# A hybrid decoder layer on one core: weight splits three chunks ahead and behind the background steps, new first and last jobs, mLSTM gates moved up

## The chip, the cores and the metric

The kernel runs on one core of one Trainium2 chip. The metric is the time of one execution on the device in microseconds; each kernel is executed several times and the median is compared.

## The reference

One inference step of one decoder layer for 256 prompt tokens and 64 sample tokens (8 sequences of 8), 320 columns in all, D = 2048, float32. Cut to what matters here:

```python
def trunk(x, ...):
    for l in range(DEPTH):                                   # DEPTH = 1
        x = x + 0.5 * swiglu(rmsnorm(x, ln_ffa[l]), w_ffa_in[l], w_ffa_out[l])   # D_FF = 5632
        y, st_new = token_mixer(rmsnorm(x, ln_mix[l]), w_in[l], ...)
        x = x + y
        x = x + 0.5 * swiglu(rmsnorm(x, ln_ffb[l]), w_ffb_in[l], w_ffb_out[l])
    return rmsnorm(x, ln_f), stacked

def token_mixer(h, ...):
    qk_pre, mv, mo, mif, aq, ak, av, gm, ga = split_cols(h @ w_in)
    qk, conv_new = causal_conv(qk_pre, conv_buf, conv_w, conv_b)      # then SiLU: mLSTM q and k
    hm, (C1, n1, m1) = mlstm(mq, mk, mv, ig, lf, C0, n0, m0)          # ig, lf from mif
    hm = sigmoid(mo) * rms(hm) * m_norm
    ha = dilated_attention(aq, ak, av, caches, biases)
    merged = sigmoid(gm) * (hm @ w_pm) + sigmoid(ga) * (ha @ w_pa)
    return merged @ w_out, new_states
```

Beside the output it returns the new keys and values, the mLSTM states and the convolution rows.

## The kernel before, in words

Activations stand feature-major: a tile holds 2 x 128 features by 320 tokens. Every weight is used once, so each product of the layer is a stream of weights through TensorE with 320 columns of activations. To keep float32 accuracy both operands are split into two reduced-precision parts, `hi` and `lo`, and each product becomes three: hi with x's high part, hi with x's low part, lo with x's high part (L144 is the helper `mm` that issues them, so all matmuls have that line; L332 is the transpose helper).

The work is a list of jobs (`add_job`), each one block of 256 output features over all its k-tiles, accumulated in a PSUM pair `fg` (two buffers). A job is cut into *chunks* of four k-tiles (512 KB of weights), numbered through the program as `ci`. The order of the jobs: first feed-forward (in blocks of 12, 12, 10 and 10 k-tiles: gate and up jobs, then eight output jobs), the mixer's projections (attention q, k, v of head pairs; the gate job `mif`, which is a single chunk with 8 columns; then for each mLSTM head v, q, k and the output gate `mo`; then 16 jobs of the branch gates), the two branch projections (`pm`, `pa`), the output projection, and the second feed-forward.

`run_job` issues a job chunk by chunk. For chunk ci it does, in this order: `split_upto(ci + HLB)`, which has ACT cast raw to `hi` (L223) and DVE subtract to `lo` (L224); one step of the background generators in the list `even` or `odd` (every second chunk each), of `slow` (8 of 15 chunks) and of `every`; the job's `setup`; in the first chunk `flush_evac`, which starts the evacuation of the job before and puts what is left of it (after its first `yield`) into `every`; `load_upto`, which issues the weight DMAs on SP; and then the chunk's 24 products. So evacuations, attention, mLSTM and conversions stand as small steps between the chunks, on all engines, and each engine works in the order of the program. HLB = 3 buffers of hi and lo and RAWB = 4 of raw mean: at chunk ci chunk ci+2 is split, into the buffer of chunk ci-1, and the load of chunk ci+6 is issued, into the buffer of chunk ci+2.

The background generators that matter here: `sample_attention` (`slow`: it transposes cache keys `kraw` on DVE into `kd`, L631, and multiplies with small matmuls), `prompt_attention` (`even`), `mlstm` (`odd`: `load_head`, `prep`, `front`, `update`, then four times `retrieve` and `state`, then `numer`), `mif_evac` (a chain of operations on 4 partitions, L814 to L876), `mv_evac`, `ak_evac`, `av_evac` (L395 `times_rstd` on DVE, then after two yields six transposes and copies: `tok_major`), `qk_evac`, and `sigmoid_evac` (DVE multiply L395, ACT exp L954, POOL add L955, and DVE reciprocals L958 after a `yield` each). `take` splits the branch results of the four heads into `bh` and `bl` (L1301, L1302) at the first `pm` and `pa` job, the first head's being made ahead by `presplit`.

The start: `load_x` and `load_upto` load four pieces of x (512 KB and the sample rows) and the first chunks in turn on SP; `prep_pair` transposes 256 features of x, and makes high and low parts with the gain; `first_chunk` places the pairs before and inside the first three chunks, with eight warm-up matmuls (`warm(8)`) before the first product. The end: the last job's evacuation, square sums over tokens by matmuls with ones (`token_sums`), square root and reciprocal, six transposes, and the scaling of the output `Y` (L1595 on ACT, L1597 on DVE), stored in six DMAs on SP.

Of the kernel before, what the change touches and what calls it, by code (L numbers as in the profile page):

```python
# [128 lines left out]
def decoder_kernel(tc, I, O, K):  # L129
# [55 lines left out]
    RAWB, HLB, KRB = 4, 3, 3  # L185
# [84 lines left out]
    def run_job(job):  # L270
        cs, nkt, mov, evac, kind, setup = job
        ps = fg_tile()
        for n, (ci, k0, nk) in enumerate(cs):
            run_later()
            if ci < 5:
                first_chunk(ci, 0)
            else:
                split_upto(ci + HLB)
# [10 lines left out]
            if n == 0 and setup is not None:  # L289
                setup()  # L290
            if ci == 7 or (n == 0 and ci != 4):
                flush_evac()
            load_upto(ci + HLB + RAWB)
            h, l = wh.pop(ci), wl.pop(ci)
            for m in range(1 if kind == "mif" else 2):
                if m and ci < 3:
                    first_chunk(ci, 1)
# [107 lines left out]
    xl = {}  # L405

    def load_x(c):
        xl[c] = fp.tile([128, 3, 512], F32, tag="xl", bufs=3, name="xl")
        G.memset(xl[c][64:128, 2], 0.0)
        dma(xl[c][:, 0:2], I["x_prompt"][0].rearrange("(t p) d -> p t d", p=128)[:, :, c * 512:(c + 1) * 512])  # L410
        dma(xl[c][0:NS, 2], I["x_sample"].rearrange("b t d -> (b t) d")[:, c * 512:(c + 1) * 512])
# [194 lines left out]
    def sample_attention():  # L606
# [145 lines left out]
        for u in range(17):  # L752
# [6 lines left out]
            if u:  # L759
                if u % 4 == 1:  # L760
                    o4 = mxt([128, 4, 128], "o", 2, "osb")
# [42 lines left out]
    def mif_evac(ps):  # L804
# [5 lines left out]
        rst = mp_tile("rst")[0:4, :, 0:NT]  # L810
# [156 lines left out]
    def mlstm():  # L967
# [229 lines left out]
        for h in range(4):  # L1197
            for s4 in range(4):
# [13 lines left out]
                elif h < 3:  # L1212
# [68 lines left out]
    add_job(w_in, 0, 16, C_MIF, mov_x, mif_evac, kind="mif")  # L1281
# [25 lines left out]
    def presplit(key):  # L1307
        while key not in M:
            yield
        PRE[key] = split_act(M[key][0], t_tile)  # L1310

    def take(key):
        for h in range(4):
            BH[h], BL[h] = PRE[key] if h == 0 and key in PRE else split_act(M[key][h], t_tile)
# [83 lines left out]
    def token_sums(x):  # L1398
        ps = bg_tile()
        for t, t0 in enumerate(TOK):  # L1400
            for m in range(2):
                mm(ps[:, t:t + 1], x[:, m, t0:t0 + 128], ones[:, 0:1], m == 0, m == 1)
        return ps


    def ffb_last(ps, j):
# [3 lines left out]
        if j < 7:  # L1410
            V.scalar_tensor_tensor(X[j], ps[:, :, 0:NT], 0.5, X[j], op0=OP.mult, op1=OP.add)
            sumsq(X[j], j, p)
        else:
            Y["sq"] = ft_tile("sq")
            for m in range(2):
                V.scalar_tensor_tensor(X[j][:, m], ps[:, m, 0:NT], 0.5, X[j][:, m], op0=OP.mult, op1=OP.add)
                S.activation(Y["sq"][:, m], X[j][:, m], AF.Square)
# [5 lines left out]
        if j < 7:  # L1423
            yield
        if j == 6:
            pa_ = token_sums(state["ss"])
            V.tensor_copy(rt, pa_[:, 0:3])
# [25 lines left out]
    vps = bg_tile()  # L1453
    tr(vps[:, 0:16], vffa)
    V.tensor_copy(gv[:, 0:16], vps[:, 0:16])

    def prep_pair(j, fg=False):
# [3 lines left out]
        ft = fg_tile() if fg else None  # L1461
        ps = [ft[:, 0], ft[:, 1]] if fg else [bg_tile(), bg_tile()]
# [4 lines left out]
        V.tensor_copy(X[j][:, 1], ps[1][:, 0:NT])  # L1467
        for m in range(2):
            S.activation(XH[j][:, m], ps[m][:, 0:NT], AF.Copy, scale=gv[:, g0 + m:g0 + m + 1])
            if m == 0:  # L1470
                S.copy(X[j][:, 0], ps[0][:, 0:NT])
        for m in range(2):
            V.scalar_tensor_tensor(XL[j][:, m], ps[m][:, 0:NT], gv[:, g0 + m:g0 + m + 1],
                                   XH[j][:, m].bitcast(F32), op0=OP.mult, op1=OP.subtract)

    def first_chunk(n, m):
        if n == 0 and m == 0:
            prep_pair(0)
            prep_pair(1)
            split_upto(1)  # L1480
            prep_pair(2, True)
            warm(8)
        elif n < 3:
            prep_pair(2 * n + 2 + m)
            if m == 1:
# [147 lines left out]
```

## Time and profile before

| | us |
|---|---|
| runs of the kernel before: median (lowest to highest) of 3 | 2980.31 (2979.14 to 2981.5) |
| the profiled execution's own time | 2975.59 |
| its span | 2973.8 |
| busy in it: PE / DVE / ACT / POOL | 2924.8 / 1637.5 / 1087.8 / 226.0 |
| mean granted clock of TensorE | 0.995 |
| DMA, mean over the span | 187 GB/s |

A page or an answer of the trace gives times from the span's start in microseconds, and mean durations in nanoseconds. "PE" is the matmuls, "PEld" the weight loads, which overlap them. In a timeline a row is: start, duration, engine, line, operation, output<-inputs, shape, how many were merged, and in brackets the idle time of the engine before it with what ended it. In a group row it is: busy us, mean ns of one, then idle time before and what ended it.

### The profile page before, as it was taken

Reading aid. Unit: us, or ns where it says so; the run is one execution under the profiler, and the core shown is the slowest. Engines: PE = TensorE matmul, PEld = TensorE weight load, DVE = VectorE, ACT = ScalarE, POOL = GpSimd, SP = SyncE. Lnnn points to the kernel's source line nnn. Section 1 sums busy time; section 2 is a strip of 40 time slices with the busy share of each in tenths; the row PEclk is TensorE's granted clock in tenths of the full one; section 3 lists DMA queues with packets and bytes.
Section 4 is the critical chain, followed back from the end, with each engine's and each line's share of the span. In section 5 each row is a group of like instructions: output and inputs, shape, how many; then the busy total and the mean of one; then the engine's idle time right before and its main releaser. Section 6 shows DMA issues by size and latency. Waiting matters only on the chain.

```text
span 2973.8 us, 51323 instructions
## 1 busy us (share of the span) xinstructions
PE 2924.8 (98%) x21538; PEld 2875.4 (97%) x21538; DVE 1637.5 (55%) x1939; ACT 1087.8 (37%) x1359; POOL 226.0 (8%) x256
## 2 busy tenths in 40 slices
PE   9999999999999999999999999999999999999998
PEld 8999999999999999988889999999999999999998
DVE  6444444444446556878888875654444444444444
ACT  5332333333334333433443443334333333333334
POOL 1000000000000000122222210000000000000000
PEclk9999999999999999999999999999999999999999
DMA  6454444444546788898999986554444444445443
GB/s 195 151 159 155 149 149 149 149 150 143 158 145 184 224 231 248 223 296 272 301 282 313 308 275 218 184 176 152 150 149 149 149 149 150 151 146 156 149 141 115
DMA packets 507477, 557.23 MB, mean 187 GB/s; under 512 B 30125, under 2 KB 452061, under 8 KB 507221
## 3 DMA queue, kind: packets, MB, share of 16 engines
q1 hardware_dynamic: 507068, 553.87, 61.2%
q8 instruction: 169, 2.77, 0.4%
q14 instruction: 64, 0.52, 0.1%
q10 hardware_dynamic: 176, 0.07, 0.0%
HBM read 521.58 MB, written 32.28 MB: 186 GB/s over the span
## 4 chain that ended last, share of the span: by engine, by line
PE 50%; DMA 1%; DVE 1%; issue 0%; ACT 0%; DVEq 0%; SPq 0%; ACTq 0%
PE fg L144 47%; PE bg L144 3%; PE bg L332 0%; DMA raw<-in_w_in_dram 0%; DMA vt<-in_cache_v_dram 0%; DMA k<-qk_d 0%; DMA raw<-in_w_pm_dram 0%; DVE kd L631 0%; DVE lo L224 0%; DVE pre L928 0%; ACT hi L223 0%; DVE sg L958 0%; DVE vs L1073 0%; DVE Y L1597 0%; DVE bl L1302 0%
## 5 line engine op out<-in xcount | busy, mean ns | idle before, releaser
L224 DVE TENSOR_TENSOR lo<-raw,hi 128x1024 fp32r<-128x1024 f32 (+1 forms) x784 | 969.1, 1237 | 1204.2 <-ACT hi L223 1189.9
L144 PE MATMUL fg<-xh,hi 128*128 128x320 f32 x4240 | 1323.0, 312 | 2.6 <-ACT hi L223 2.6
L144 PE MATMUL fg<-xh,lo 128*128 128x320 f32 x4240 | 1314.3, 310 | 8.6 <-DVE lo L224 8.6
L144 PE MATMUL fg<-xl,hi 128*128 128x320 f32 x4240 | 1313.0, 310 | 0.0
L223 ACT CAST hi<-raw 128x1024 fp32r<-128x1024 f32 (+1 forms) x784 | 806.3, 1029 | 1356.7 <-PE fg L144 1014.2
L144 PEld LDWEIGHTS fg<-xh,lo 128*128 128x128 f32 x4240 | 797.4, 188 | 11.7 <-DVE lo L224 11.5
L144 PEld LDWEIGHTS fg<-xh,hi 128*128 128x128 f32 x4240 | 797.9, 188 | 5.7 <-ACT hi L223 3.1
L144 PEld LDWEIGHTS fg<-xl,hi 128*128 128x128 f32 x4240 | 797.8, 188 | 1.0 <-issue 0.2
L144 PE MATMUL fg<-hh,hi 128*128 128x320 f32 x1408 | 437.0, 310 | 0.0
L144 PE MATMUL fg<-hl,hi 128*128 128x320 f32 x1408 | 435.2, 309 | 0.0
L144 PE MATMUL fg<-hh,lo 128*128 128x320 f32 x1408 | 435.2, 309 | 0.0
L144 PEld LDWEIGHTS fg<-hl,hi 128*128 128x128 f32 x1408 | 264.4, 188 | 0.7 <-issue 0.7
L144 PEld LDWEIGHTS fg<-hh,hi 128*128 128x128 f32 x1408 | 264.4, 188 | 0.7 <-issue 0.7
L144 PEld LDWEIGHTS fg<-hh,lo 128*128 128x128 f32 x1408 | 264.4, 188 | 0.0
L439 POOL TENSOR_TENSOR gt<-gt,rstd 128x640 f32<-128x640 f32 x44 | 69.2, 1573 | 1876.8 <-ACT gt L438 1876.8
L144 PE MATMUL fg<-bl,hi 128*128 128x320 f32 x512 | 158.5, 310 | 1.9 <-DVE bl L1302 1.9
L144 PE MATMUL fg<-bh,hi 128*128 128x320 f32 x512 | 158.7, 310 | 1.5 <-ACT bh L1301 1.5
L144 PE MATMUL fg<-bh,lo 128*128 128x320 f32 x512 | 158.3, 309 | 0.0
L631 DVE STREAM_TRANSPOSE kd<-kraw 128x512 f32<-128x512 f32 x160 | 101.2, 677 | 10.8 <-DMA kraw<-in_cache_k_dram 10.8
L144 PEld LDWEIGHTS fg<-bl,hi 128*128 128x128 f32 x512 | 96.1, 188 | 2.4 <-DVE bl L1302 2.4
L144 PEld LDWEIGHTS fg<-bh,hi 128*128 128x128 f32 x512 | 96.1, 188 | 2.2 <-ACT bh L1301 2.0
L144 PEld LDWEIGHTS fg<-bh,lo 128*128 128x128 f32 x512 | 96.1, 188 | 0.0
(295 smaller groups left out, 1495.7 us busy)
## 6 DMA issues: line engine op xcount, KB each, us to landing
raw<-in_w_ffa_in_dram SPq DMA_DIRECT2D x176, 512.0 KB
raw<-in_w_in_dram SPq DMA_DIRECT2D x176, 512.0 KB
raw<-in_w_ffb_in_dram SPq DMA_DIRECT2D x176, 512.0 KB
raw<-in_w_ffa_out_dram SPq DMA_DIRECT2D x80, 512.0 KB
raw<-in_w_ffb_out_dram SPq DMA_DIRECT2D x80, 512.0 KB
kraw<-in_cache_k_dram SPq DMA_DIRECT2D x96, 256.0 KB
vt<-in_cache_v_dram SPq DMA_DIRECT2D x128, 192.0 KB
kraw<-in_cache_k_dram SPq DMA_DIRECT2D x32, 512.0 KB
```

What stands on the lines that cost most here:

```text
L144: T.matmul(out, a, b, start=start, stop=stop, **kw)
L223: S.copy(hi[:, :nk], t[:, :nk])
L224: V.tensor_tensor(lo[:, :nk], t[:, :nk], hi[:, :nk].bitcast(F32), op=OP.subtract)
L439: G.tensor_tensor(gt, gt, bcast(rstd, 2), op=OP.mult)
L631: V.transpose(kd[:, 2 * pr + g], t[:, g])
```

## The change

1. HLB = 4 and RAWB = 3: chunk ci+3 is split at chunk ci, into the buffer of chunk ci-1; the load of chunk ci+6 goes into the buffer of chunk ci+3.
2. In `run_job` the order within a chunk becomes: setup, `flush_evac`, the steps, then the split, then the loads and the products. A generator that `flush_evac` starts so gets its second part in the same chunk.
3. The start: the sample rows are loaded on ACT's queue; the first x piece and the first weight chunk are loaded in halves in turn; each pair of x tiles is followed by half a chunk's split; the first four chunks' products are ordered by pair (four hi-high, four hi-low, four lo-high), with the next pair's transposes behind them; the eight warm-up matmuls go; vectors, tables and states are loaded some chunks later.
4. The end: the last job runs its two halves of 128 features one after the other (`run_last`), so that the first half's sums and transposes stand inside the second's products. Scaling is split over DVE (first 128 tokens), ACT (second) and POOL (sample rows), the last 128 features are scaled straight from PSUM, and ACT issues its own stores.
5. The `mif` job moves from behind the four head pairs to behind the first.
6. `load_head` of the next head comes at the third of four state steps instead of the last; two heads are split ahead by `presplit` instead of one; two 512-column key transposes become one of 1024; `osb` has one buffer instead of two; `rst` takes another pool's tile.

The diff, cut to its core:

```diff
-    RAWB, HLB, KRB = 4, 3, 3
+    RAWB, HLB, KRB = 3, 4, 3
...
             run_later()
-            if ci < 5:
-                first_chunk(ci, 0)
-            else:
-                split_upto(ci + HLB)
+            if n == 0 and setup is not None:
+                setup()
+            if ci == 7 or (n == 0 and ci != 4):
+                flush_evac()
             if tick[0] % 2 == 0:
                 step(even)
...
             step(every)
-            if n == 0 and setup is not None:
-                setup()
-            if ci == 7 or (n == 0 and ci != 4):
-                flush_evac()
+            if ci > 3:
+                split_upto(ci + HLB)
+            if ci < 4:
+                first_chunk(ci, ps)
+                load_upto(ci + 1 + RAWB)
+                continue
             load_upto(ci + HLB + RAWB)
...
-            for g in range(2):
-                V.transpose(kd[:, 2 * pr + g], t[:, g])
+            V.transpose(kd[:, 2 * pr:2 * pr + 2].rearrange("p a b -> p (a b)"), t.rearrange("p a b -> p (a b)"))
...
-        rst = mp_tile("rst")[0:4, :, 0:NT]
+        rst = m3_full("rst").rearrange("p a b -> p (a b)")[0:4, 0:2 * NT].rearrange("p (a n) -> p a n", a=2)
...
-                elif h < 3:
+                if s4 == 2 and h < 3:
                     while M["qk"] < 2 * (h + 2):
                         yield
                     load_head(h + 1)
...
-    add_job(w_in, 0, 16, C_MIF, mov_x, mif_evac, kind="mif")
+        if p == 0:
+            add_job(w_in, 0, 16, C_MIF, mov_x, mif_evac, kind="mif")
...
-        PRE[key] = split_act(M[key][0], t_tile)
+        for h in range(2):
+            PRE[key, h] = split_act(M[key][h], t_tile)
+            yield
...
+    def last_sum(ps, m):
...
+        V.scalar_tensor_tensor(x, ps[:, 0, 0:NT], 0.5, x, op0=OP.mult, op1=OP.add)
+        S.activation(Y["sq"][:, m], x, AF.Square)
+        S.activation(Y["xn"][:, m], x, AF.Copy, scale=gv[:, c:c + 1])
...
+    def run_last(job):
+        cs, nkt, mov, evac, kind, setup = job
+        for m in range(2):
+            ps = fg_tile()
+            for n, (ci, k0, nk) in enumerate(cs):
+                run_later()
+                split_upto(ci + HLB)
+                step(every)
+                if m == 0 and n == 0:
+                    flush_evac()
+                if m == 1 and n == 1:
+                    sp = token_sums([(state["ss"], 0), (state["ss"], 1), (Y["sq"], 0)])
+                    V.tensor_copy(rt, sp[:, 0:3])
+                    a = last_tr(0)
...
-    for c in range(4):
-        load_x(c)
+    load_x(0, S)
+    load_x(1, S)
+    load_x(2, S)
+    raw[0] = wp.tile([128, 4, 256], F32, tag="raw", bufs=RAWB, name="raw")
+    for a in range(2):
+        load_xp(0, 256 * a, 256 * a + 256)
+        dma(raw[0][:, 2 * a:2 * a + 2], chunks[0][0][:, 2 * a:2 * a + 2])
+    st["loaded"] = 1
+    for c in (1, 2):
+        load_xp(c, 0, 512)
         load_upto(c + 1)
-    load_vecs()
+    load_upto(4)
+    load_x(3)
+    load_xp(3, 0, 512)
...
+        for pair in (2 * n, 2 * n + 1):
+            k0 = 2 * (pair % 2)
+            for which in range(3):
+                for m in range(2):
+                    for k in range(k0, k0 + 2):
...
+            if pair < 6:
+                prep_pair(pair + 2)
+            elif pair == 6:
+                split_upto(6)
...
+    for c0, c1, c2 in ((0, 1024, 1024), (1024, 1920, D)):
+        for t in (0, 1, 2):
...
+            if c2 > c1:
+                scale(y[:, c1:c2], a[r0:128, t * 128:(t + 1) * 128], S if t == 1 else V)
+            scale(y[:, c0:c1], y[:, c0:c1], (V, S, G)[t])
+            (S if t == 1 else nc.sync).dma_start((ypv[:, t] if t < 2 else ysv)[:, c0:c2], y[:, c0:c2])
```

Where instructions move, first TensorE at the program's start, before (numbers behind names tell tiles apart; rows with `ident` and `xl` are the transposes of x, those with `ones` the warm-up, `fg` with `xh`, `xl`, `hi`, `lo` the first products):

```order
L144 MATMUL bg_137<-ones_72 128x128 x9
L332 MATMUL bg_147<-ident_71,vffa_100 128x16
L332 MATMUL bg_154<-ident_71,xl_106 128x128 x3
L332 MATMUL bg_155<-ident_71,xl_106 128x128 x3
L332 MATMUL bg_171<-ident_71,xl_106 128x128 x3
L332 MATMUL bg_172<-ident_71,xl_106 128x128 x3
L332 MATMUL fg_192<-ident_71,xl_112 128x128 x6
L144 MATMUL bg_205<-ones_72 128x128 x8
L144 MATMUL fg_150<-xh_152,hi_185 128x320
L144 MATMUL fg_150<-xl_153,hi_185 128x320
L144 MATMUL fg_150<-xh_152,lo_186 128x320
```

and TensorE at the same place after:

```order
L144 MATMUL bg_133<-ones_72 128x128 x9
L334 MATMUL bg_147<-ident_71,xl_106 128x128 x3
L334 MATMUL bg_148<-ident_71,xl_106 128x128 x3
L334 MATMUL bg_155<-ident_71,vffa_100 128x16
L334 MATMUL bg_171<-ident_71,xl_106 128x128 x3
L334 MATMUL bg_172<-ident_71,xl_106 128x128 x3
L144 MATMUL fg_143<-xh_145,hi_162 128x320 x4
L144 MATMUL fg_143<-xl_146,hi_162 128x320 x4
L144 MATMUL fg_143<-xh_145,lo_163 128x320 x4
L334 MATMUL bg_202<-ident_71,xl_109 128x128 x3
L334 MATMUL bg_203<-ident_71,xl_109 128x128 x3
```

Ahead of the first product now stand two pairs of transposes (six each) instead of three and no second warm-up; four products with the same kind of operands stand in a row, and the next pair's transposes behind them.

Next DVE where the first mLSTM head's v is evacuated (`mv`), before; the `rows`, `mnew` and `RT` rows are the gate chain of `mif_evac`, and L558 belongs to the prompt attention:

```order
L840 SCALAR_TENSOR_TENSOR rows_11021<-rst_11022,rows_11021 4x320
L224 TENSOR_TENSOR lo_11224<-raw_11029,hi_11223 128x1024
L843 TENSOR_TENSOR rows_11019<-rows_11020,rows_11021 4x320
L845 COPY mnew_8967<-rows_11019 4x1
L846 COPY mnew_8967<-rows_11019 4x8
L850 COPY RT_8968<-rows_11021 4x1
L851 COPY RT_8968<-rows_11021 4x8
L395 TENSOR_TENSOR mv_11233<-fg_11007,rstd_76 128x640
L224 TENSOR_TENSOR lo_11262<-raw_11089,hi_11261 128x1024
L558 TENSOR_TENSOR s_11268<-bg_11265,tp_11172 128x128
```

and DVE at the same evacuation after:

```order
L754 STREAM_TRANSPOSE sm_9011<-sm_9011 128x32
L636 STREAM_TRANSPOSE kd_9009<-kraw_11057 128x1024
L224 TENSOR_TENSOR lo_11207<-raw_11066,hi_11206 128x1024
L397 TENSOR_TENSOR mv_11242<-fg_11052,rstd_76 128x640
L224 TENSOR_TENSOR lo_11245<-raw_11120,hi_11244 128x1024
L564 TENSOR_TENSOR s_11277<-bg_11274,tp_11193 128x128
```

The gate chain is gone from here. The `lo` behind `mv` is the split at the end of the same chunk after, and that at the start of the next chunk before.

Last DVE at an output gate (`sg`, with the reciprocals of `sigmoid_evac` on `sg` and of `qk_evac` on `pre`; `C` is the mLSTM state, `kd` the key transposes), before:

```order
L395 TENSOR_TENSOR sg_12849<-fg_12586,rstd_76 128x640
L224 TENSOR_TENSOR lo_12881<-raw_12684,hi_12880 128x1024
L631 STREAM_TRANSPOSE kd_9007<-kraw_12714 128x512 x2
L928 RECIPROCAL pre_12628<-pre_12628 128x320
L958 RECIPROCAL sg_12849<-sg_12849 128x320
L224 TENSOR_TENSOR lo_12919<-raw_12748,hi_12918 128x1024
```

and after:

```order
L397 TENSOR_TENSOR sg_12818<-fg_12591,rstd_76 128x640
L1128 SCALAR_TENSOR_TENSOR C_12441<-C_12441,sTb_8973,bg_12826 128x512
L933 RECIPROCAL pre_12600<-pre_12600 128x320
L963 RECIPROCAL sg_12818<-sg_12818 128x320
L224 TENSOR_TENSOR lo_12839<-raw_12682,hi_12838 128x1024
L636 STREAM_TRANSPOSE kd_9009<-kraw_12711 128x1024
```

The first reciprocal of `sg` stood a chunk behind the multiply, with a split between the two; now both stand in one chunk, ahead of its split.

More of the change, by code (lines that the diff above doesn't have):

```diff
@@ L1502, in first_sumsq @@
             yield
-        rstd_now()
     def init_tables():
-        yield
+        for _ in range(6):
+            yield
         tab = fp.tile([128, TABW], F32, name="tab")
```

140 lines of the change are left out of this document (82 added, 58 removed).

## The prediction

> **What bounds the kernel now.** I read the page first, then busy time by stretch, then what TensorE waited for, then the timeline at both ends. A *chunk* is four k-tiles of weights: 24 products with 320 columns, split by ACT and DVE into hi and lo before TensorE uses them. The page's first lines:
>
> ```profile
> span 2973.8 us, 51323 instructions
> PE 2924.8 (98%) x21538; PEld 2875.4 (97%) x21538; DVE 1637.5 (55%) x1939; ACT 1087.8 (37%) x1359; POOL 226.0 (8%) x256
> ```
>
> TensorE is busy 98% of the span, so only its idle time, its throttled time and its extra work can be won. Busy time by stretch (stretch, its length, then busy us and count of PE, PEld, DVE, ACT, POOL, granted clock, DMA share, GB/s):
>
> ```profile
> 60.00:900.00 840.00, 840.00 (x5713) 835.86 (x5712) 371.52 (x342) 275.70 (x283) 38.14 (x32) 1.00 0.49 151
> 900.00:2010.00 1110.00, 1080.29 (x8989) 1038.67 (x8989) 794.53 (x1146) 443.29 (x660) 149.21 (x191) 0.99 0.83 249
> 2010.00:2940.00 930.00, 929.78 (x6345) 929.33 (x6344) 420.87 (x385) 322.55 (x345) 34.70 (x22) 1.00 0.48 149
> 1175.00:1200.00 25.00, 21.32 (x139) 20.98 (x138) 20.36 (x42) 11.16 (x20) 0.39 (x1) 0.93 0.88 271
> 1275.00:1300.00 25.00, 21.82 (x239) 19.60 (x238) 12.54 (x27) 8.30 (x14) 0.62 (x4) 0.93 1.03 280
> 1300.00:1325.00 25.00, 23.35 (x148) 21.99 (x147) 23.58 (x45) 11.28 (x22) 8.81 (x12) 0.93 1.02 305
> 1325.00:1350.00 25.00, 22.32 (x229) 20.31 (x231) 22.13 (x22) 9.33 (x14) 8.37 (x10) 0.93 0.93 266
> 1400.00:1425.00 25.00, 21.24 (x139) 19.91 (x138) 22.10 (x36) 12.71 (x20) 8.47 (x13) 1.00 1.03 302
> 1625.00:1650.00 25.00, 24.87 (x256) 22.89 (x257) 19.21 (x33) 14.74 (x23) 8.46 (x14) 0.93 1.00 287
> 1500.00:1800.00 300.00, 292.24 (x2648) 276.66 (x2650) 249.81 (x324) 127.45 (x194) 69.96 (x76) 0.99 0.96 293
> ```
>
> The two feed-forward stretches have no idle time to give: 840 us hold 5713 matmuls, 147 ns each, and a chunk takes 24 x 0.147 = 3.53 us there. The mixer between them leaves 1110 - 1080.3 = 29.7 us idle. Five stretches of it show a clock of 0.93, and 0.07 x 25 = 1.75 us are lost in each, 8.75 us together. TensorE's waits in the mixer (total, times, longest):
>
> ```profile
> PE fg L144 <- DVE lo L224: 6.7, 8, 2.4
> PE bg L332 <- DVE mv L395: 6.0, 3, 3.7
> PE bg L144 <- DMA k<-qk_d: 3.3, 1, 3.3
> PE bg L144 <- POOL ks L1021: 3.0, 3, 2.2
> PE bg L332 <- issue: 2.8, 1, 2.8
> PE fg L144 <- ACT hi L223: 2.3, 1, 2.3
> PE fg L144 <- DVE bl L1302: 1.9, 2, 1.0
> PE fg L144 <- ACT bh L1301: 1.5, 2, 0.7
> PE bg L144 <- POOL qm L1010: 1.2, 2, 0.6
> ```
>
> They sum to 28.7 us. So three places can pay: the start, the mixer, the end.
>
> **The change part by part.** *Start.* TensorE's rows of the start, and the ACT and DVE groups that prepare one pair of x tiles (with the half-size casts, taken from the last stage, where they occur):
>
> ```profile
> 5.95 1.70 PE L332 MATMUL bg<-ident,xl 128*128 128x128 f32 x12
> 9.25 0.44 PE L332 MATMUL fg<-ident,xl 128*128 128x128 f32 x2 [1.59 <-DMA xl<-in_x_prompt_dram]
> 13.40 0.61 PE L144 MATMUL fg<-xh,hi 128*128 128x320 f32 x1
> 34.61 0.43 PE L332 MATMUL bg<-ident,vrow 112*128 112x112 f32 x2
> L1469 ACT ACTIVATE xh<-bg,gv 128x320 fp32r<-128x320 f32 x14 | 7.3, 527 | 10.0 <-PE bg L332 8.0 <-DVE x L1467 1.8
> L1473 DVE SCALAR_TENSOR_TENSOR xl<-bg,gv,xh 128x320 fp32r<-128x320 f32 x14 | 7.6, 549 | 0.6
> 2929.48 0.62 ACT L223 CAST hi<-raw 128x512 fp32r<-128x512 f32 x1 [0.89 <-ACT Y L1436]
> 2930.13 0.69 DVE L224 TENSOR_TENSOR lo<-raw,hi 128x512 fp32r<-128x512 f32 x1 [0.30 <-ACT hi L223]
> ```
>
> Before, the first product runs at 13.40, behind three pairs of transposes, a whole chunk's split and eight warm-up matmuls; chunk 3 ends at 34.61. The rate of the DMA engines in the first 45 us, in 40 slices of 1.125 us:
>
> ```profile
> GB/s 0 56 268 260 216 346 363 279 293 373 341 252 365 373 235 311 114 330 105 335 56 0 0 47 314 105 0 0 46 325 423 423 315 178 352 319 218 306 234 266
> ```
>
> With the second x piece 1.77 MB have been asked for; the slices reach that at 8.1, and it was there at 9.25, 1.1 later. After, pair 0 needs half an x piece (0.26 MB), its sample rows (0.13) and ident (0.07): 0.46 MB, reached at 3.7, there at 4.8. Half a weight chunk (0.26 more) is there at 5.9. Ahead of the first product in TensorE's order stand pair 1's transposes, with another 0.26: 0.98 MB, reached at 5.9, there at 7.0. Pair 0's chain from 4.8: transposes 0.85, a gain table of perhaps 0.4, two scales 2 x 0.53, half a cast 0.62: 7.7. Pair 1's transposes end at 7.9, and the first product follows. Then eight pairs of 12 products (12 x 0.147 = 1.76 us each) and six more sets of transposes (0.85 each, half of the 1.70): 14.1 + 5.1 = 19.2, so chunk 3 ends at 27.1, 7.5 earlier. DVE needs 2 x 0.55 + 0.69 and a copy for a pair, ACT 2 x 0.53 + 0.62 and a copy, both under TensorE's 2.6 us. I take 7, since each pair hangs on a chain over three engines. Bounds: 3 if the data pace it, 10 if half the transposes overlap. The sample loads move to ACT's queue, ahead of its table load; ACT is not needed there before pair 0's scales. The vector, table and state loads move later in SP's queue, past the weights; nobody reads them before the end of the first feed-forward, so I cost them at nothing.
>
> *Mixer, the split.* With four hi/lo buffers a split waits for the release of the chunk before last, one chunk (3.53 us) earlier than now. It stands behind the steps of its chunk, which is the same place in ACT's and DVE's order as "ahead of the next chunk's steps" two ahead, so nothing is put in front of it; only its wait is looser. The weight load loses one buffer: load n waits for split n-3, not n-4, but that split may come a chunk earlier, so the load starts when it did. Behind a waiting load on SP stand the cache and state loads. Every wait for lo or hi in the table is at most 2.4 us, shorter than 3.53: of 9.0 us I take 7.5.
>
> *Mixer, gates moved up.* The longest mv wait (3.7) falls, by the order, where the gate chain's small operations stand on DVE just ahead of mv; they move to a place with less DVE work. But evacuations now go ahead of the steps and their generators take one step in the same chunk, so the mv transposes come one chunk earlier. Of 6.0 I take 4.5.
>
> *Mixer, the rest.* The next head's load one step pair earlier: of 3.3 + 2.8 (the second ends in krep, which waits for the same k) I take 5.5. Two heads split ahead: TensorE reaches the third head's tiles a chunk later, so all of 1.9 + 1.5 = 3.4 goes. POOL's ks and qm, 4.2: a side effect, 1.5. One transpose for two saves DVE a fixed cost, nothing on TensorE. Sum of waits: 7.5 + 4.5 + 5.5 + 3.4 + 1.5 = 22.4.
>
> *Mixer, clock.* The five 0.93 stretches all hold one of these waits. The Trainium skill (TensorE: Matmul & The Clock Gate, section "Why this matters for your kernels") says to have no PE-idle gap over about 3 us; by that rule only the gaps of 3.7 and 3.3 would throttle, and 3.5 us would be the most to win. The trace differs: only two waits of the table are longer than 2.8, yet five stretches throttle, and 1400 to 1425, with 3.8 us idle in all, does not. I take three of the five, 5.2 us.
>
> *Mixer, against it.* The sigmoid jobs (16 branch gates, 4 output gates) now have their first reciprocal in the chunk of their evacuation, so DVE stands until ACT and POOL are done:
>
> ```profile
> L954 ACT ACTIVATE sg<-sg 128x640 f32<-128x640 f32 x20 | 14.8, 738 | 67.8 <-DVE sg L395 67.8
> L955 POOL TENSOR_SCALAR sg<-sg 128x640 f32<-128x640 f32 x20 | 36.3, 1814 | 140.1 <-ACT sg L954 105.3 <-issue 29.9 <-PE bg L144 4.9
> 1521.39 0.78 DVE L395 TENSOR_TENSOR sg<-fg,rstd 128x640 f32<-128x640 f32 x1
> ```
>
> That is up to 0.74 + 1.81 = 2.55 us, 20 times, 51 us of DVE. The 16 branch gates begin at 1521, in a stretch where DVE is busy 249.8 of 300. Queued behind the waiting reciprocal are the split and, a chunk on, the evacuations that the transposes need. Other steps fill part of the wait and the lead covers the rest: of 51 I charge 8 to TensorE. Mixer: 22.4 + 5.2 - 8 = 19.6.
>
> *End.* From the last product on:
>
> ```profile
> 2958.89 0.31 PE L144 MATMUL fg<-hh,lo 128*128 128x320 f32 x1
> 2959.23 0.89 DVE L1416 SCALAR_TENSOR_TENSOR x<-fg,x 128x320 f32<-128x320 f32 x2 [1.33 <-PE fg L144]
> 2960.34 1.64 PE L144 MATMUL bg<-ones,sq 128*128 128x1 f32 x12 [1.14 <-ACT sq L1417]
> 2962.74 1.54 DVE L1597 TENSOR_SCALAR Y<-Y,rt 128x1024 f32<-128x1024 f32 x2
> 2967.74 1.30 SPq L141 DMA_DIRECT2D out_y_sample_dram<-Y  x1
> 2965.00:2966.00 1.00, 0.00 (x0) 0.00 (x0) 0.97 (x2) 0.54 (x1) 0.00 (x0) 0.50 1.00 406
> L925 POOL TENSOR_SCALAR pre<-pre 128x640 f32<-128x640 f32 x8 | 6.0, 750 | 55.1 <-ACT pre L924 46.2 <-PE fg L144 9.0
> ```
>
> The scaling starts 3.5 us after the last product's end (2959.2), the last store is issued 8.5 after it, and the span ends 14.6 after it. One half of the job alone then costs one 0.45 update instead of two and half the sums: scaling at about 2.5. But the stores still move 2.6 MB, 6.5 us at 406 GB/s, and the sample rows go through POOL, 1024 and 896 elements: 2.9 + 2.5 us by L955's rate, 1.2 + 1.1 by L925's. By the first the last store is issued 7.9 after the last product, by the second at about 6; I take the first, its form is the nearer (one operation, not two). That is 0.6 to 2.5 earlier, with less backlog ahead of it about 2 us, and three sums and three transposes (0.7 us) now run ahead of the last product: net 1.5, bounds -1 and 4. The Trainium skill (SBUF — State Buffer, "Who interferes with whom") has VectorE and GpSimd share a port pair that one holds for a whole instruction. By that rule POOL's first scale could hold DVE's up to 2.9 us and the end would gain nothing; the gap between 1814 and 750 ns for one size agrees with some such blocking and does not show whose.
>
> **How the numbers follow.** 7 + 19.6 + 1.5 = 28 us. The profiled execution took 2975.6 (1.8 beside its span) and would take 2947.5; the median of the runs is 4.7 higher, and I keep that: 2980.3 - 28 = 2952.3. Chance 0.56 for this, within 22 to 38 us gained.
>
> **Rivals.** *The lead is not there to be used* (0.20): splits run ahead only if the weights have landed, and one raw buffer less may turn the wait for TensorE into a wait for the transfer. For it: a DMA share of 1.02 to 1.03 in three of the stretches. Against: 0.83 over the mixer, and loads that start no later. Splits and clock pay nothing (7.5 + 5.2): 15 gained, 2965. *Everything goes* (0.15): start 8, 28.7 of waits, 8.75 of clock, end 1.5, 3 charged back: 44 gained, 2936. *DVE becomes the bound* (0.05): if the 2.55 us stand unfilled 20 times and DVE has no room, TensorE pays 51 in place of the 8: 28 + 8 - 51 = 15 slower, 2995. It decides where a gate job's DVE room is below 2.55: over 1500 to 1800 it has 50.2 / 16 = 3.1 us, so the mean speaks against it and a burst for it. Between that and the first rival lies a draw (0.04).
>
> About 0.2% (6 us) can be told from no change here. The range leaves out DVE as the bound, the draw, and the edges of the first two rivals: 2936 to 2968. Faster 0.91, same 0.04, slower 0.05.
>
> **What would show it.** Right: chunk 4 begins near 27; no TensorE waits for lo, hi, bh, bl or k<-qk_d in the mixer; fewer stretches at 0.93; scaling about 2.5 us after the last product. Wrong: DVE idle behind POOL's sg with TensorE waiting for lo or mv between 1500 and 1800; ACT's hi waiting for raw's transfer, and TensorE for hi behind it; a span over 2968.

## The result, and the profile after

The changed kernel takes 3025.62 us (median of 4 runs, 3024.62 to 3027.34), the kernel before on the same chip 2979.86 (2979.14 to 2981.5): a ratio of 1.0153, 95% interval 1.0136 to 1.0171. It is 46 us slower; I had forecast 28 faster. The profiled execution took 3025.41 us.

The page of the kernel after, its first lines (span, then busy time and share of the span):

```profile
span 3023.5 us, 51193 instructions
PE 2938.0 (97%) x21522; PEld 2887.9 (96%) x21522; DVE 1647.0 (54%) x1863; ACT 1083.2 (36%) x1364; POOL 222.1 (7%) x258
```

Every engine has about the work it had. Busy time by stretch, in the columns of the prediction's rows:

```profile
60.00:900.00 840.00, 840.00 (x5712) 835.63 (x5711) 378.63 (x345) 276.89 (x287) 37.41 (x29) 1.00 0.48 153
900.00:2010.00 1110.00, 1041.33 (x8629) 998.96 (x8628) 767.01 (x1036) 418.44 (x634) 140.28 (x194) 0.97 0.80 241
2010.00:2940.00 930.00, 929.54 (x6337) 929.12 (x6336) 424.98 (x380) 315.29 (x331) 34.67 (x22) 1.00 0.47 151
1375.00:1400.00 25.00, 16.17 (x95) 15.76 (x95) 11.86 (x19) 8.18 (x14) 1.46 (x2) 0.80 0.95 274
1500.00:1525.00 25.00, 11.23 (x114) 10.77 (x116) 11.56 (x15) 5.58 (x8) 3.11 (x3) 0.66 0.85 249
```

The feed-forward stretches are as before. In the mixer TensorE is busy 1041.3 of 1110 us instead of 1080.3, at a mean clock of 0.97 instead of 0.99, and DMA moves less (241 GB/s, 249 before): nothing is at its limit, things wait. If the products with 320 columns are counted in both traces, the 6,000th starts 3.1 us earlier than before, the 11,000th, behind the mixer, 49.8 later, and the span ends 49.7 later (3023.5 - 2973.8). So the mixer lost 53 us, and start and end together gained 3. Most of the 53 is idle time: between the same two products TensorE idles 28.8 us before and 68.7 after, 40 more. The rest is throttled clock. The records of the granted clock hold 17 us at half rate in the mixer before and 68 after, but 21.6 of the 68 fall into idle time and cost nothing; half of what is left is lost, 8.3 us before and 23.3 after, 15 more. (Idle time and clock sum to 55 by this count, in which the ends of the matmuls are modelled.) What TensorE waited for (total, times, longest):

```profile
PE bg L144 <- POOL ks L1026: 37.1, 6, 13.8
PE fg L144 <- DVE lo L224: 10.0, 7, 2.7
PE bg L144 <- POOL qm L1015: 7.1, 3, 3.7
PE bg L334 <- DVE k L397: 3.8, 1, 3.8
PE bg L334 <- DVE mv L397: 3.4, 1, 3.4
```

The wait for `ks` was 3.0. Why ks is late stands in ACT's waits: more waits for weights, and two rows for `isb`, the copy of the retrieved state, which waited for no transfer before (run 13 below tests that this is the cause).

The row of the kernel before:

```profile
ACT hi L223 <- DMA raw<-in_w_in_dram: 48.3, 16, 9.0
```

The rows of the kernel after:

```profile
ACT hi L223 <- DMA raw<-in_w_in_dram: 159.5, 50, 10.7
...
ACT isb L1119 <- DMA out_C_sample_dram<-C: 23.3, 2, 17.6
ACT isb L1119 <- DMA raw<-in_w_in_dram: 14.7, 1, 14.7
```

The timeline of the kernel after around the first such wait, on ACT:

```profile
1385.41 0.37 ACT L1119 COPY isb<-bg 128x256 f32<-128x256 f32 x1 [17.55 <-DMA out_C_sample_dram<-C]
1385.68 0.51 ACT L1024 ACTIVATE ks<-kr,eb 128x256 fp32r<-128x256 f32 x1
1386.21 0.50 ACT L1025 ACTIVATE kf<-kr,eb 64x256 f32<-64x256 f32 x1
```

The same place on POOL:

```profile
1386.85 0.72 POOL L1026 TENSOR_TENSOR ks<-kf,ks 64x256 fp32r<-64x256 f32 x1 [14.71 <-issue]
```

And on TensorE:

```profile
1387.63 0.80 PE L144 MATMUL bg<-vs,ks 128*128 128x256 f32 x2 [8.83 <-POOL ks L1026]
1388.22 0.47 PE L144 MATMUL fg<-xh,hi 128*128 128x320 f32 x1
1388.49 0.47 PE L144 MATMUL fg<-xl,hi 128*128 128x320 f32 x1
...
1392.75 0.31 PE L144 MATMUL fg<-xh,lo 128*128 128x320 f32 x1
1392.90 0.30 PE L144 MATMUL fg<-xh,hi 128*128 128x320 f32 x1
```

The reader should read this downwards: ACT stands 17.55 us in front of a copy of 0.37 us, because the slot of its ring still holds a C tile whose store has not landed. What stands behind the copy in ACT's order, the scaling of ks, needs none of that and is late with it; POOL adds it up, and TensorE, with products ready behind it, stands 8.83 us. When it comes back its products follow each other at 0.27 us, half rate, for 5 us, instead of 0.147.

The two ends, kernel after: the first transposes and the first product, the start of chunk 4, then the last product and the first scaling:

```profile
7.12 1.09 PE L334 MATMUL bg<-ident,xl 128*128 128x128 f32 x4 [1.51 <-DMA xl<-in_x_sample_dram]
10.17 1.44 PE L144 MATMUL fg<-xh,hi 128*128 128x320 f32 x4
30.27 0.41 PE L144 MATMUL fg<-xh,hi 128*128 128x320 f32 x1 [0.22 <-ACT hi L223]
3009.90 0.31 PE L144 MATMUL fg<-hh,lo 128*128 128x320 f32 x1
3012.89 0.75 DVE L1671 TENSOR_SCALAR Y<-Y,rt 128x1024 f32<-128x1024 f32 x1
```

Chunk 4 began at 34.97 before. The first scaling comes 2.7 us after the last product's end (3.5 before), and the span ends 13.3 after it (14.6).

### The profile page after: what moved, and what is told of

It reads as the page before. It is cut to its first block, busy times and chain, and to the rows that moved or that the text cites. A ratio compares the mean times of both kernels' runs of the same rounds, so it can differ in the third digit from the quotient of the medians.

```text
span 3023.5 us, 51193 instructions
## 1 busy us (share of the span) xinstructions
PE 2938.0 (97%) x21522; PEld 2887.9 (96%) x21522; DVE 1647.0 (54%) x1863; ACT 1083.2 (36%) x1364; POOL 222.1 (7%) x258
## 4 chain that ended last, share of the span: by engine, by line
PE 80%; issue 6%; DMA 6%; DVE 4%; SPq 1%; ACT 1%; POOL 0%; POOLq 0%; ACTq 0%; DVEq 0%
PE fg L144 77%; PE bg L144 3%; DMA raw<-in_w_in_dram 2%; DMA kraw<-in_cache_k_dram 2%; DVE lo L224 1%; SPq L141 1%; DMA vt<-in_cache_v_dram 1%; PE bg L334 1%; DVE y L925 1%; DVE kd L636 0%; ACT hi L223 0%; DVE pre L933 0%; DMA raw<-in_w_pm_dram 0%; DVE sg L963 0%; DMA out_C_sample_dram<-C 0%
## 5 line engine op out<-in xcount | busy, mean ns | idle before, releaser
L636 DVE STREAM_TRANSPOSE kd<-kraw 128x1024 f32<-128x1024 f32 x80 | 96.4, 1219 | 8.7 <-DMA kraw<-in_cache_k_dram 8.7
```

The source lines that it names most:

```text
L636: V.transpose(kd[:, 2 * pr:2 * pr + 2].rearrange("p a b -> p (a b)"), t.rearrange("p a b -> p (a b)"))
```

## The experiments

All times are medians, ratios are to the kernel before on the same chip. "Theory A" of the first group is that the early head load, by the slot of `isb`, costs most of the 46 us. The letters of the later groups are explained in their expectations.

**1. Head load back at its old step.** In the changed kernel:

```
-                if s4 == 2 and h < 3:
+                elif h < 3:
```

> The changed kernel with the next head's load back at the last of the four state steps, nothing else undone. Theory A (the early head load takes a slot of the nine-tile ring m2, so that the copy isb on ACT waits for a state tile's store; seen 17.6 + 14.7 + 5.7 = 38 us of ACT, and behind it 8.8 + 13.8 + 7.0 us of TensorE waiting for ks, plus the throttled stretches): about 2985 us (2975 to 2995), no wait of isb for a transfer. Rival B (the loss is spread over split, flush order and weight transfers, with isb only where it shows): above 3010 us.

Measured: 3015.05 us, ratio 1.0121 (1.0103 to 1.0139). The waits of isb for transfers are gone but for 1.1 us, yet only 10 us come back. Theory A falls as the main cause. TensorE's waits are now spread over many names, and ACT's waits for weights stay:

```profile
ACT hi L223 <- DMA raw<-in_w_in_dram: 179.5, 57, 9.7
```

TensorE's longest waits in the same kernel:

```profile
PE fg L144 <- DVE lo L224: 10.9, 10, 2.6
PE bg L144 <- DMA k<-qk_d: 10.1, 2, 7.4
...
PE bg L144 <- POOL ks L1026: 6.6, 3, 4.2
```

**2. The early head load alone.** In the kernel before:

```
-                elif h < 3:
+                if s4 == 2 and h < 3:
```

> The kernel before with the early head load alone. Theory A: slower by 25 to 45 us, 3005 to 3025, and isb on ACT waits for transfers by over 20 us in all. Rival B: the load alone is harmless or gives the 6 us that the prediction counted, 2972 to 2985.

Measured: 2995.62 us, ratio 1.0056 (1.0038 to 1.0074): it costs some 17 us by itself, with 22.9 us of TensorE's waits for ks (3.0 before).

**3. Head load late, buffers as before.** The kernel of 1 with

```
-    RAWB, HLB, KRB = 3, 4, 3
+    RAWB, HLB, KRB = 4, 3, 3
```

> As the first, with three hi/lo and four raw buffers again (split two ahead, in the new place behind the steps). If the third chunk of lead is worth what the prediction took (7.5 us of waits, some clock): 6 to 12 us slower than the first. If the weights' transfers take the lead away (the first rival of the prediction): within 4 us of the first, or faster.

Measured: 3007.37 us, ratio 1.009 (1.0068 to 1.0112). Without the lead of three chunks the kernel is, if anything, faster (the intervals overlap). ACT's waits for weights fall to 63.5 us, and TensorE waits for lo instead (26.2 us, 21 times). So something that is left in this kernel costs 27 us and is neither the head load nor the lead.

**4. The slot of isb taken ahead of the early head load.** The changed kernel, with for h < 3

```
+                    H[h]["isb"] = m2_tile("isb")[:, 0:256]
                     load_head(h + 1)
```

> The changed kernel with the early head load kept, and the tile isb taken from the ring ahead of that load. Theory A by the slot: isb no longer waits; about 2980 to 2995. If not the slot but the early traffic costs the time: still over 3005. If the wait only moves, to the load of vq on SP's queue: between, 2995 to 3010, with SP standing ahead of vq.

Measured: 3026.97 us, ratio 1.0168 (1.0141 to 1.0195): no change. The copy still waits for stores, 42 us in all: the slot one place earlier in the ring holds a C tile too. This run tells nothing about whether the slot is the way; run 13 does.

**5. Split ahead of the steps, lead kept.** The kernel of 1 with the split moved from behind the steps to just ahead of them (setup and evacuation stay in front):

```
             if ci == 7 or (n == 0 and ci != 4):
                 flush_evac()
+            if ci > 3:
+                split_upto(ci + HLB)
             if tick[0] % 2 == 0:
...
-            if ci > 3:
-                split_upto(ci + HLB)
```

> The changed kernel with the head load back at its old step and the split put ahead of the background steps of each chunk, right behind the evacuation; the lead of four split buffers and three weight buffers stays. Theory B (the split stands behind a block's background steps on VectorE, so the weight load that waits for it on SP, and the mixer's loads queued behind that load, come late): about 2985, ScalarE's waits of hi for weights back from 180 to near 50 us. Theory C (the gates' job at its new place, with the tiles that it shifts, costs it): no change from the 3015 of the kernel with only the head load put back, hi's waits still over 150 us. Theory D (the order of evacuation and setup ahead of the steps costs it): 3005 to 3015 too, hi's waits down.

Measured: 3000.27 us, ratio 1.0072 (1.005 to 1.0094): 15 us come back, half of what theory B expects, and ACT's waits for weights stay at 140.0 us, which it does not expect. A part of the loss must lie elsewhere.

**6. The old order inside a chunk** (split, steps, setup, evacuation) and the old buffers, head load late. Of the change stay the start, the end, the gates' place, two heads split ahead, the single transposes:

```
-            if n == 0 and setup is not None:
-                setup()
-            if ci == 7 or (n == 0 and ci != 4):
-                flush_evac()
+            if ci > 3:
+                split_upto(ci + HLB)
...
+            if n == 0 and setup is not None:
+                setup()
+            if ci == 7 or (n == 0 and ci != 4):
+                flush_evac()
```

> The changed kernel with the head load at its old step, four weight buffers and three split buffers as before, and the old order inside a chunk: split, background steps, setup, evacuation. What stays of the change is the start, the end, the gates' job at its new place, two heads split ahead and the single transposes. Theory B: about 2976, below the kernel before by the start and end (some 4 us). Theory D: also about 2976. Theory C: 3000 to 3008, since the same buffers with the split behind the steps gave 3007.

Measured: 2967.96 us, ratio 0.9967 (0.9954 to 0.998): 9.5 us *faster* than the kernel before, and the fastest kernel of the study. I call it the base below. Its mixer:

```profile
900.00:2010.00 1110.00, 1085.73 (x9035) 1043.92 (x9034) 792.81 (x1068) 445.29 (x663) 149.11 (x194) 0.99 0.84 251
```

**7. The base with the gates' job at its old place** (and its tile and the buffers of o as before):

```
-        if p == 0:
-            add_job(w_in, 0, 16, C_MIF, mov_x, mif_evac, kind="mif")
+    add_job(w_in, 0, 16, C_MIF, mov_x, mif_evac, kind="mif")
```

> As the one with the old order inside a chunk, and the gates' job back behind the last value job, with its tile and the buffers of o as before. Theory B: as that kernel, 2976 within 3. Theory C: 2974 to 2978, and that is 25 us below the same kernel with the gates' job moved.

Measured: 2972.29 us, ratio 0.998 (0.997 to 0.9989). Theory C (the gates cost it) falls: their new place, with the tiles that go with it, saves some 4 us, with intervals that overlap.

**8. The split behind the steps and the evacuation, alone.** The kernel before, from chunk 5 on:

```
-            else:
-                split_upto(ci + HLB)
...
+            if ci > 4:
+                split_upto(ci + HLB)
```

> The kernel before with one edit: from chunk 5 on, the split stands behind the background steps and the evacuation of its chunk instead of ahead of them; all else, buffers too, as before. Theory B: 2995 to 3010, ScalarE's waits of hi for weights from 48 to over 100 us. Theories C and D: 2978 to 2984, since neither the gates nor the order of evacuation and steps is touched.

Measured: 3011.87 us, ratio 1.0113 (1.0098 to 1.0128): this one move costs 34 us. The size is just above theory B's range, the way only partly its own. ACT's waits for weights are 49.4 us, not over 100; TensorE waits for lo (before: 6.7 in the mixer):

```profile
PE fg L144 <- DVE lo L224: 38.1, 29, 9.0
PE bg L144 <- DMA k<-qk_d: 11.7, 2, 6.8
```

The longest of them in the timeline, on DVE:

```profile
1288.93 0.71 DVE L631 STREAM_TRANSPOSE kd<-kraw 128x512 f32<-128x512 f32 x1 [14.39 <-DMA kraw<-in_cache_k_dram]
...
1290.52 1.18 DVE L224 TENSOR_TENSOR lo<-raw,hi 128x1024 fp32r<-128x1024 f32 x1
```

On TensorE:

```profile
1291.76 0.63 PE L144 MATMUL fg<-xh,lo 128*128 128x320 f32 x1 [9.03 <-DVE lo L224]
```

DVE stands 14.39 us for cache keys, and the split, now behind that step, stands with it. The base has such a wait too, with the split ahead of it, and TensorE's longest wait for lo there is 3.5. DVE's row in the base:

```profile
DVE kd L636 <- DMA kraw<-in_cache_k_dram: 12.3, 1, 12.3
```

SP, where the next loads queue behind a weight load that waits for lo, stood in front of one for at most 6.0 us in the kernel before:

```profile
SPq L141 <- DVE lo L224: 1922.3, 684, 6.0
```

And for up to 10.6 us with the split behind the steps:

```profile
SPq L141 <- DVE lo L224: 1976.1, 669, 10.6
```

**9. The base with the lead** (three weight and four split buffers, the split at the head of the chunk):

```
-    RAWB, HLB, KRB = 4, 3, 3
+    RAWB, HLB, KRB = 3, 4, 3
```

> The 2968 us kernel (old order inside a chunk, head load at its old step) with the changed kernel's buffers: three for weights, four for splits, so that the split runs three chunks ahead, at the head of the chunk. Theory E (a weight load that waits for a buffer that one split later frees has a chunk less before its own split stands on ScalarE, and what stands behind that split there is late): 2985 to 2995, ScalarE's waits of hi for weights from 47 to some 140 us. Theory D (evacuation and setup ahead of the steps cost it): 2964 to 2970, since that order is the old one here. The prediction's credit of 7.5 us for the lead would give 2960.

Measured: 2995.0 us, ratio 1.0059 (1.0044 to 1.0074): 27 us slower than the base, as theory E has it. ACT's waits for weights in the base:

```profile
ACT hi L223 <- DMA raw<-in_w_in_dram: 46.6, 18, 7.4
```

In this kernel:

```profile
ACT hi L223 <- DMA raw<-in_w_in_dram: 184.7, 52, 12.2
```

TensorE's longest waits:

```profile
PE bg L144 <- POOL qm L1015: 9.6, 6, 4.0
PE bg L144 <- POOL ks L1026: 7.3, 3, 3.4
PE bg L144 <- ACT kw L1082: 6.5, 2, 4.6
```

No wait for lo is left in the first rows: the lead does what it is for. But ACT, in order, stands at hi for weights that are still on their way, and what stands behind it, kw and the parts of qm and ks, is late instead. From the starts of SP's load instructions and of the casts that read them (1100 to 1850 us), a load has a median of 12.9 us from issue to cast in the base and 9.7 here; where the cast waited for it, the load had taken a median of 9.5 and 8.9. Three us of slack became less than one.

**10. The base with setup and evacuation ahead of split and steps.**

> Setup and evacuation ahead of the split and of the background steps as in the changed kernel, the split ahead of the steps, four weight and three split buffers, head load at its old step: the 2968 us kernel with setup and evacuation moved to the head of the chunk. Theory D: 2985 to 2995. Theory E: 2966 to 2972.

Measured: 2977.65 us, ratio 0.9996 (0.9987 to 1.0006): 9.7 us slower than the base, outside both theories' ranges. Theory D holds for about ten, not for 17 to 27. DVE does not stand in the sigmoid jobs here, as the prediction feared: its waits have no row for sg behind POOL, in this kernel as in the base. That row comes only where the split stands behind the steps as well, in the changed kernel (runs 1, 3 and 4 have it with 14.5 to 15.2):

```profile
DVE sg L963 <- POOL sg L960: 15.1, 11, 2.7
```

With the split ahead of the steps, a split stands on DVE between the multiply of sg and its first reciprocal. TensorE's longest waits end in ACT's kw. TensorE's rows of this run:

```profile
PE bg L144 <- ACT kw L1082: 6.0, 1, 6.0
...
PE bg L334 <- ACT kw L1082: 5.7, 1, 5.7
```

**11. The base with the early head load** (the edit of 2).

> The 2968 us kernel with the early head load of the changed kernel alone. Theory F (the early load takes slots of the mixer's tiles ahead of the state steps' own, so that the copy of the state waits for the store of the tile that stood in its slot): 2980 to 2987, as the early load alone cost the kernel before 17 us. The prediction's credit: 2963 to 2966.

Measured: 2985.04 us, ratio 1.0025 (1.0015 to 1.0034): 17 us, as in run 2. What the copy isb waited for:

```profile
  DMA out_C_sample_dram<-C: 33.2, 3
```

And TensorE's longest row:

```profile
PE bg L144 <- POOL ks L1026: 20.6, 6, 10.4
```

**12. The base with four weight and four split buffers**, and two for the raw keys to make room (`RAWB, HLB, KRB = 4, 4, 2`).

> The 2968 us kernel with four weight buffers and four split buffers, which leaves two buffers instead of three for the raw keys of the cache: the lead of three chunks without the lost weight buffer. Theory E: 2962 to 2970 and ScalarE's waits of hi for weights at 50 us or under, unless the keys' third buffer is needed, which would show as waits of VectorE's transposes for the keys. If the lead itself costs (splits early stand in other work's way): 2975 and above with hi's waits low.

Measured: 2974.71 us, ratio 0.9987 (0.9978 to 0.9997). With the weight buffer given back ACT's waits for weights are 42.1 us, so theory E holds; the 7 us above the base are the keys' buffer or the lead, which run 14 separates.

**13. The early head load, with isb in a buffer of its own.** The kernel of 11 with

```
-                d["isb"] = m2_tile("isb")[:, 0:256]
+                d["isb"] = mxt([128, 256], "isb", 1, "isb")
```

> The 2968 us kernel with the early head load, and the copy of the retrieved state (isb) in a buffer of its own instead of a slot of the mixer's ring of nine. Theory F (the early load costs because the state copy, shifted along the ring, waits for the store of C): the waits of isb for stores go, and the time comes back to 2965 to 2972. Rival G (the early load costs because its transfers crowd the queue ahead of weights and values, wherever the copy lies): 2980 to 2987, with waits for another transfer in the place of isb's.

Measured: 2972.23 us, ratio 0.9983 (0.9974 to 0.9992). The waits of isb are gone, and 13 of the 17 us with them: theory F. TensorE's wait for ks falls from 20.6 to

```profile
PE bg L144 <- POOL ks L1026: 2.7, 3, 2.1
```

**14. The base with two key buffers** (`RAWB, HLB, KRB = 4, 3, 2`).

> The 2968 us kernel with two buffers for the raw keys instead of three, all else the same: the other half of the run with four weight and four split buffers (2975). If the keys' third buffer made that run slower: 2973 to 2978, VectorE's waits for keys near 35 us as there. If a lead of three chunks itself cost it: 2967 to 2970.

Measured: 2974.82 us, ratio 0.999 (0.998 to 0.9999), the same as run 12, with the same wait for keys:

```profile
DVE kd L636 <- DMA kraw<-in_cache_k_dram: 35.2, 9, 18.2
```

So the lead of three chunks, with no weight buffer lost for it, neither gains nor costs (2974.71 against 2974.82, both with two key buffers). With run 9 this says that it is the lost weight buffer that costs; a kernel with three weight buffers and no lead was not run.

**15. The base with isb in its own buffer**, the head load late.

> The 2968 us kernel with the state copy in its own buffer and the head load at its old step: what the buffer does without the early load. Theories F and G: 2964 to 2970, since the copy waited for no store at its old slot; the ring's slots behind it shift, which may cost a few us of its own.

Measured: 2969.43 us, ratio 0.9971 (0.9961 to 0.998): the same as the base. Run 13 is 2.8 above it, with intervals that overlap: the early load itself brings nothing that can be told once its side effect is taken away.

The way from the base to the changed kernel, one edit at a time, by ratios: 0.9967 (base), 1.0059 with three weight buffers (+27 us), 1.0072 with setup and evacuation first (+4), 1.0121 with the split behind the steps (+15), 1.0153 with the early head load (+10). In another order the same edits weigh differently: setup and evacuation first +9, the split behind +28, the lead +9. The +4 and the +9 of the lead come with intervals that overlap. That the edits share one loss, since each delays the same engines in order, is my reading and not shown.

## Why the prediction was wrong

The mixer was to become 19.6 us faster and became 53 slower. **The step that failed most** is in the mixer's split: "The weight load loses one buffer: load n waits for split n-3, not n-4, but that split may come a chunk earlier, so the load starts when it did." With the split at the head of the chunk (run 9) the load may start when it did; what I left out is that the split which needs it also comes a chunk earlier. Run 9 shows it: 12.9 us from issue to cast become 9.7, the load takes about 9, and ACT's waits for weights go from 46.6 to 184.7 us. I had the rival in hand (*the lead is not there to be used*) and named the sign, "ACT's hi waiting for raw's transfer". I priced it as a gain that stays away, 15 instead of 28. It is a cost, since everything behind hi on ACT is late as well: 27 us.

**The sentence before it fails too**, on the split behind the steps. I wrote that it is "the same place in ACT's and DVE's order as 'ahead of the next chunk's steps' two ahead, so nothing is put in front of it". That holds for the order on DVE and ACT at four buffers. It does not hold for SP: the load waits for that split, so load ci+6 now goes out behind all of chunk ci's steps instead of ahead of them. Run 8 shows what a step that waits for a transfer does to a split behind it, at the old lead: 34 us. Between runs 5 and 1, with the lead, it is 15. That part of this goes through SP's queue is argued from the longer waits there (6.0 before, 10.6 in run 8, 11.3 after) and not shown alone. Between runs 5 and 1 DVE's 15.2 us behind POOL's sg come in too, so how the 15 divide stays open.

**The head load**, "of 3.3 + 2.8 ... I take 5.5", was a cost of 10 us in the changed kernel and 17 in the base and in the kernel before. I had counted its transfers and what waits for k, and not the tiles that it takes from a ring of nine, which moves the copy isb into the slot of a tile with a store under way. Runs 11 and 13 show this: 13 of 17 us go with a buffer of its own. The 5.5 was not there either: run 13 is no faster than run 15.

**The split's credit of 7.5** was not there to be won with this: runs 12 and 14 are equal. The waits for lo did become fewer (17.8 us in run 14, 12.7 of it one wait, and 3.5 in run 12), but others grew (qm from no row to 7.2, cs from 3.4 to 4.9).

**The charge of 8 against it**, for evacuations ahead of the steps and DVE standing in the sigmoid jobs, is near the 9.7 of run 10, but by luck: the evacuations ahead of the steps cost that much there without any wait of DVE for POOL's sg, the thing that I had charged. What makes up the 9.7 stays open; the longest waits end in ACT's kw. In the changed kernel DVE did stand, 15.1 of the 51 us that I had bounded, and what this cost TensorE was not measured alone.

**The start**, taken at 7, gave 4.7 at chunk 4 (30.27 instead of 34.97) and 3.1 in the end. My chain from the data to the first product had the right length, 3.1 us expected and 10.17 - 7.12 = 3.05 measured. The data were 2.3 late: TensorE's first transposes for the sample columns waited for the sample rows, whose loads the change moves to ACT's queue, a move that I had charged nothing for.

**Gates, presplit, transposes.** The gates' new place saves about 4 (runs 6 and 7; I took 4.5); the base's waits for mv are 2.1, with the old place 5.6. Two heads split ahead: bh and bl wait 1.7 in the base instead of 3.4, half of what I took.

**The end**, net 1.5: the tail shortens by 1.3, though not by an earlier last store, as I had it (issued 8.8 after the last product, 8.5 before, 7.9 expected), and the work moved ahead of the last product costs about as much (the last product is 51.0 later than before, the 18,000th 50.0). Net nothing, within my bounds of -1 and 4.

**The clock**, credited with 5.2, went the other way: it loses 23.3 us in the mixer instead of 8.3. In the base, with shorter waits, it loses 6.8. So the sign of this term hangs on the waits, which were forecast wrong.

The base shows that the parts outside the order of the chunks do gain: 9.5 us, where my terms for start, gates, presplit, end and the loose side effect on ks and qm sum to 7 + 4.5 + 3.4 + 1.5 + 1.5 = 17.9, the clock left aside. By the count of products the base is 3.2 us ahead of the kernel before at the 6,000th and 9.9 at the 11,000th: 6.7 come in the mixer and nothing at the end.

## What to carry to other kernels

A lead of one more chunk costs a load its slack if the buffer for it is taken from the loads: count the time from the issue of a transfer to its reader, and compare it with the transfer's duration, before and after. On an engine that works in order, an instruction that waits early is a wait for everything behind it, so work that feeds the bottleneck belongs ahead of steps that may wait for transfers. A load moved earlier also takes its tiles from rings earlier; look whose slot the next users get, and whether a store still reads it.

## What the runs showed of the hardware

In the mixer half rate came in pieces of 3.4 us and whole multiples: in the kernel after, the records last 3.41, 6.83, 10.24 and 17.07 us. Such a piece can begin while TensorE still waits: with the waits of 8.83 and 13.8 us for ks it began 5.1 and 11.2 us before TensorE's return, and TensorE then ran at half rate for another 5 and 6 us. In the same kernel, a wait of 3.4 us for mv (1452) left the clock at 1.00 over 1440 to 1465, with 5.2 us idle in that stretch, while one of 3.8 for k (1155) gave 0.86:

```profile
1150.00:1175.00 25.00, 21.22 (x233) 19.68 (x233) 11.11 (x20) 7.97 (x16) 1.30 (x1) 0.86 0.96 241
1440.00:1465.00 25.00, 19.78 (x224) 18.20 (x228) 17.62 (x22) 5.46 (x8) 2.84 (x5) 1.00 0.91 294
```

So a bound on a single gap (the Trainium skill, TensorE: Matmul & The Clock Gate, has about 3 us in "Why this matters for your kernels") does not sort these rows: a gap of 2.6 us for qm (1700) went with half rate, and so did one of 1.0 us for lo in the kernel before (1321), while the one of 3.4 us did not.

At the end POOL's scale of 64 by 1024 took 3.25 us, by its group in the kernel after:

```profile
L1671 POOL TENSOR_SCALAR Y<-Y,rt 64x1024 f32<-64x1024 f32 x1 | 3.3, 3252 | 90.9 <-PE bg L334 90.9
```

It began at 3013.11. DVE's row beside it:

```profile
3013.82 1.28 DVE L1671 TENSOR_SCALAR Y<-Y,rt 128x896 f32<-128x896 f32 x1
```

DVE's 896 columns beside it took 1.28 us. Its 1024 columns just before, from 3012.89, took 0.75, so 896 would take some 0.66 at that rate. By the rule of the shared port pair (the Trainium skill, SBUF — State Buffer, "Who interferes with whom") I had let DVE be held for up to 2.9 us; it was slowed by some 0.6 and, by POOL's recorded times, was done 1.3 us ahead of POOL, so the trace does not show a hold for the whole instruction.
